# Recurrent states two half products apart, a split moved, and stores on another queue in a 2112-token hybrid layer

## The chip, the cores and the metric

The kernel runs on one core of one Trainium2 chip. Its engines work side by side, each through its own list of instructions: TensorE (PE, matrix products), VectorE (DVE), ScalarE (ACT), GpSimd (POOL), and SyncE (SP), which here only issues DMAs. ACT and POOL can issue DMAs as well. An instruction waits on semaphores for what it needs, and whatever stands behind it in its engine's list waits too. The metric is the device time of one execution in microseconds (us), as a median of several.

## The reference

One layer of a decoder with `d_model` 1024, in float32, for 2048 tokens of a prompt and 64 tokens of eight samples (2112 together). Two branches read the same input: sliding-window attention, and gated linear attention (GLA) with 4 heads of key width 128 and value width 256. The branches are projected, gated and added, projected once more, and normalised.

```
z = einsum('btd,dn->btn', x, w_in)
q, k, v, g_att, gq, gk, gv, g_gla, g_lr, r_att, r_gla = split(z)
o_att = sink_softmax(q k^T / 8 + rel_bias, window 128) v
log_a = log_sigmoid(g_lr @ w_gk_up + b_gk) / 16

# GLA, per head, in chunks of tokens; b = cumsum(log_a) in the chunk
o = (q exp(b)) S + tril((q exp(b)) (k exp(-b))^T) v
S = exp(b_last) S + (k exp(b_last - b))^T v

o = o * rsqrt(mean(o^2) + eps) * gla_norm_w
merged = sigmoid(r_att) * ((o_att * silu(g_att)) @ w_pa)
       + sigmoid(r_gla) * ((o * silu(g_gla)) @ w_pg)
y = layer_norm(DN_ALPHA * x + merged @ w_o)
```

Outputs are `y`, the last window of keys and values, and the GLA state after the prompt and after each sample.

## The kernel before

**Products.** A float32 operand is kept as two parts: `hi`, a cast to a shorter float type made on ACT (L123), and `lo`, the rest, subtracted on DVE (L124). A product is three matmuls (hi·hi, hi·lo, lo·hi) for each 128 rows of the contraction: L211 to L213 in the projections, L785 to L787 in the GLA, L1351 to L1353 in the merge. Names: `x` input, `wst` a raw weight and `wh`, `wl` its parts, `pd` and `pa` PSUM buffers, `wgk` the weights of the log gates.

**Stages** in the order of time, with the 2112 tokens in six chunks of 384 (four times), 256 and 320 (of it 64 samples):

- start, to about 100 us: first loads, splits, bias tables. `setup0` to `setup3` are its parts.
- attention, to about 397: per block of 128 queries scores, softmax, `att_trans` (transposes on PE, copied from PSUM into `pT`), `att_out`.
- GLA, about 357 to 1066, head after head, in each head chunk after chunk. The gate product z = `gin`·`wgk` (`gla_z`) opens a chunk; ACT and DVE make log gates, their running sum and four Exps of it from z (two table loads of ACT among them).
- merge, about 1066 to 1649: four passes of products over the branches (`w_pa`, `w_ra`, `w_rg`, `w_pg`), each by a seven-product scheme for 2×2 blocks, with 84 groups of matmuls. The third pass makes the GLA gates: PE, then DVE adds into `fin` (six buffers), then ACT's Tanh on it, then a store to `tt_d` in memory, which the fourth pass loads again as `cs`.
- output projection and norm, to the end.

**The recurrence.** A chunk has `nt` blocks of 128 tokens (3, or 2 in the last two chunks). Each goes through three parts. `gla_a`: scores (L763) and transpose of k (L764), then four casts or subtractions `ak` on ACT and DVE that split both. `gla_b`: the old state times q (L785 to L787 on `st`), the new state from `ak` and the values, the update on DVE (`ring`, L803), its split `st`, and the norm of the block's output (ACT square L777, POOL's `sq`, ACT scale L780). `gla_c`: two transposes of the normed output (L813), and the gating on DVE (L816). `samp_a`, `samp_b` and the "s" `gla_c` do the same for the samples of the last chunk, with states `S` that are loaded from `state` and stored to `o_ss`.

**What sets the order.** PE's list is in the order in which the program is written. The parts of the recurrence are put on a side list, `at(n, part)`, and are written out at the n-th next `tick()`; ticks stand between the dense products. In the first and third head (even) a tick is one full product of 24 matmuls. In the second and fourth (odd) a product has a tick in its middle too (`mid` in `proj`), so a tick is a half product of 12 matmuls, and a chunk has 8 of them: two gate products, k and q. `chain` says at which ticks the parts of a chunk stand. The fourth head's last two chunks are interleaved (`end`): that is its tail. The lists of ACT, DVE, POOL and SP are made by a scheduler that places each instruction by the order written and by when its inputs are due; `tc.issue_after` pins an instruction behind another. So a part that moves on PE takes its helpers on the other engines with it, and may land on the other side of unrelated work there.

Of the kernel before, what the change touches and what calls it, by code (L numbers as in the profile page):

```python
# [12 lines left out]
F32 = mybir.dt.float32  # L13
# [3 lines left out]
ALU = mybir.AluOpType  # L17
# [4 lines left out]
P = 128  # L22
# [4 lines left out]
NS = NB * TS  # L27
# [9 lines left out]
GH = 4  # L37
# [20 lines left out]
def kernel(ctx, tc, io):  # L58
# [47 lines left out]
    def at(d, fn):  # L106

        while len(side) <= d:
            side.append([])
        side[d].append(fn)  # L110
# [197 lines left out]
    def setup0():  # L308

        oneh = unit(name="oneh")  # L310
        rtab = small([33, NH], "rtab", 1)
        nc.gpsimd.memset(rtab, 1.0)
        nc.gpsimd.dma_start(oneh[:33, :LB], io["c_onehot"])
        nc.gpsimd.dma_start(rtab[:32], io["rel"])
        nc.gpsimd.dma_start(sink, io["sink"].broadcast_to([P, NH]))
        ssel = unit(name="ssel")[:NH, :2 * P].rearrange("h (a p) -> h a p", a=2)
        scol = small([NH, 1], "scol", 1)
        nc.gpsimd.dma_start(ssel, io["c_ssel"])
        nc.gpsimd.dma_start(scol, io["sink"].rearrange("a h -> h a"))
        oh = unit(F32R, "oh")[:33, :LB]  # L320
        rbh, rbl = (wtile(F32R, n).rearrange("p (h q) -> p h q", h=NH)[:33] for n in ("rbh", "rbl"))
        rt = rtab.unsqueeze(2).broadcast_to([33, NH, P])
        with tc.issue_after(pin["a"].ins), tc.issue_after(pin["d"].ins):
            nc.scalar.copy(wgk, wgk_st)
            nc.vector.tensor_tensor(wgk[64:], wgk_st[64:], wgk[64:].bitcast(F32), ALU.subtract)
            nc.scalar.copy(oh, oneh[:33, :LB])
            nc.vector.tensor_copy(rbh, rt)
            nc.vector.tensor_tensor(rbl, rt, rbh.bitcast(F32), ALU.subtract)
        st1.update(oh=oh, rbh=rbh, rbl=rbl, ssel=ssel, scol=scol)
# [30 lines left out]
            st1["bias", kv] = b  # L360

    def setup3():
        flat = bs_d.rearrange("h q j -> h (q j)")
        bias_s = unit(name="bias_s")[:, :2 * (W + TS)].rearrange("p (a k) -> p a k", a=2)
        for b in range(4):
            for h in range(NH):
                r = 32 * b + 8 * (h % G)
                f = flat[h, 127:127 + TS * (LB - 1)].rearrange("(q j) -> q j", j=LB - 1)
                nc.gpsimd.dma_start(bias_s[r:r + TS, h // G, :], f[:, :W + TS])
        st1["bias_s"] = bias_s  # L370
# [66 lines left out]
    def att_trans(A, bi, kv):  # L437
        first = A["kprev"] is None and bi == 0
        s = A.pop(("s", bi, kv))
        pT = wtile(name="pT").rearrange("p (a q) -> p a q", a=2)  # L440
        for hf in range(1 if first else 0, 2):
            tp = pa()
            for g in range(G):
                nc.tensor.transpose(tp[:, g * P:(g + 1) * P], s[:, g, hf * W:(hf + 1) * W], ident)
            nc.scalar.copy(pT[:, hf], tp)
        A["pT", bi, kv] = pT

    def att_out(A, bi):
# [122 lines left out]
    R = {}  # L571
# [10 lines left out]
    for c, (t0, T) in enumerate(CHUNKS):  # L582
# [2 lines left out]
        nblk = Tp // W  # L585
        if last:
            wcap(16)
        A = {"kprev": kprev, "vprev": vprev, "q": [], "sil": []}

        def wt1(key):  # L590
            if c == 0:
# [168 lines left out]
    def gla_a(B, i):  # L760
        ts = slice(i * P, (i + 1) * P)
        ap = pa()
        mm(ap[:, :P], B["k"][:, ts], B["q"][:, ts], start=True, stop=True)  # L763
        nc.tensor.transpose(ap[:, 256:256 + P], B["k2"][:, ts], ident)  # L764
        A_ = rot("a")
        nc.vector.copy_predicated(A_, cmask.bitcast(U32), ap[:, :P])
        As = rot("As")
        split(As[0], As[1], A_)
        kT2 = rot("kT")
        split(kT2[0], kT2[1], ap[:, 256:256 + P])  # L770
        B["a", i] = (As, kT2)
# [127 lines left out]
        for n_, x_ in ((0, x1), (2, x2)):  # L899
            nc.sync.dma_start(dst[n_:n_ + 2].rearrange("n p t -> p n t"), x_.rearrange("p (n t) -> p n t", n=2))  # L900

    def chain(B, o=0, late=False):

        last, nt = B["last"], B["nt"]
        if B["h"] == 0 and B["t0"] == 0:
            rings()
        short = nt == 2 and not last and o == 0
        end = last and B["h"] == GH - 1
        for i in range(nt):
            at(o + i, lambda B=B, i=i: gla_a(B, i))  # L910
            at((3, 5)[i] if short else o + i + 2, lambda B=B, i=i: gla_b(B, i))
            if not late:
                at((6, 7)[i] if short else o + i + 4, lambda B=B, i=i: gla_c(B, i, P, i * P))
        if last:
            at(o + nt + 2, lambda B=B: (nc.gpsimd if end else nc.sync).dma_start(
                io["o_sp"][B["h"]], R["S"][sstate[B["h"]]]))
            at(o + nt - 1, lambda B=B: samp_a(B))
            at(o + nt + 1, lambda B=B: samp_b(B, 0))
            at(o + nt + 2, lambda B=B: samp_b(B, 4))
            at(o + nt + 5, lambda B=B: gla_c(B, "s", NS, B["Tp"]))  # L920
            at(o + nt + 5, lambda B=B: gla_store(B))
        elif not late:
            at(7 if short else o + nt + 4 if o else 6, lambda B=B: gla_store(B))

    def values(B, i):

# [58 lines left out]
    for h in range(GH):  # L985
        W2 = {}
        odd = h % 2

        def wt2(*key):
            if key not in W2:  # L990
                W2[key] = wget()
            return W2[key]

        for c in range(len(CHUNKS)):
            last = c == LAST
            end = h == GH - 1 and c >= LAST - 1
            if not end:
                B = chunk(h, c, gin, gvn if odd else [])
            else:
                B = Bn  # L1000

            sums = [combine_load(stile)] if c else []
            if odd and c in (1, 2):
                sums.append(combine_load(lambda n: wtile(name=n)))

            def combine():
                if sums:
                    with tc.issue_after(pin["d"].ins):
                        combine_do(*sums.pop(0), nc.vector)

            def ahead():

                nh, nx = (h, c + 1) if not last else (h + 1, 0)
                if nh == GH:
                    return None, None, None
                g = gin5.pop() if gin5 else gate_in(nh, nx)
                return tiles(load_x(nx)), g, load_v(nh, nx) if nh % 2 else []

            if not odd:
                wv = [wt2("v", i) for i in range(4)]  # L1020
                if c == 0:
                    wcap(wseq[0] + 2)
                for i in range((B["T"] + P - 1) // P):
                    values(B, i)
                    if c == 0:
                        wload()
                    tick()
                if last:
                    wcap(wseq[0] + 4)
                    wload(2)  # L1030
            xn, gin, gvn = ahead()
            if odd and not end:
                if h < GH - 1 and c == 2:
                    wcap(wseq[0] + 6)
                for m in range(2):
                    gates(B, x, m, True)
                    if last:
                        wload()
                if 1 < c:
                    wload()  # L1040
            if h == GH - 1 and LAST - 2 <= c < LAST:
                Bn = chunk(h, c + 1, gin, gvn)
                if c == LAST - 2:
                    gin5.append(gate_in(h, LAST))
            dense(B, x, wt2("k"), gla_k, odd)
            combine()
            if not odd and last:
                wload()
            tick()
            dense(B, x, wt2("q"), gla_q, odd)  # L1050
            if not odd and last:
                wload()
            tick()
            combine()
            if end and not last:
                B["keep"] = wtile(name="keep")
                chain(B, 1, late=True)
                Bg, xg = B, x
            elif end:
                chain(B)  # L1060
                for m in range(2):
                    gates(B, x, m, True)
                for m in range(2):
                    gates(Bg, xg, m, True)
                for i in range(Bg["nt"]):
                    gla_c(Bg, i, P, i * P)
                drain()
                gla_store(Bg)
            else:
                if not odd:  # L1070
                    for m in range(2):
                        gates(B, x, m, False)
                chain(B, 1 if (h if not last else h + 1) % 2 else 0)
            x = xn


# [137 lines left out]

    def gate_sink(z, parts, ct, ts):
        nc.scalar.activation(z, z, AF.Tanh, scale=0.5)
        nc.sync.dma_start(tt_d[:, ct, 0, ts], z)

    def merge_sink(z, parts, ct, ts):
        nc.vector.scalar_tensor_tensor(z, parts[0], 1.0, z, ALU.add, ALU.mult)  # L1220
# [337 lines left out]
```

## Time and profile before

| | |
|---|---|
| median of 3 runs | 1852.0 us (1847.4 to 1854.77) |
| profiled execution | 1853.14 us |
| its span (first to last instruction) | 1851.4 us |
| granted TensorE clock | 0.991 |
| PE busy | 1806.5 us, 98% |
| DVE, ACT, POOL busy | 64%, 42%, 21% |
| DMA | mean 209 GB/s |

How to read it: a row of the timeline has the start and duration in us, the engine, the source line, the operation, `output<-input` by the program's names, shapes, and in square brackets the engine's idle time before it with what ended it. The rows of waits give the total, the number and the longest. A row of DMA issues gives the issuing engine's time; "to landing" is from the issue until the data has arrived. A releaser is inferred from semaphore events. Matmuls are pipelined and their ends are modelled, so two neighbours overlap in the list; the time from start to start is the measured one.

### The profile page before, as it was taken

What the parts mean: (1) busy time and instruction counts of PE and PEld (TensorE: products, weight loads), DVE (VectorE), ACT (ScalarE), POOL (GpSimd) and SP (SyncE); (2) the same over time, 40 slices, a digit from 0 to 9 for tenths busy, and PEclk for the clock granted to TensorE, in tenths of its full rate; (3) what the DMA queues carried; (4) which work ended last, traced back from release to release, by engine and by line L of the source; (5) the groups of instructions that cost most, each with busy time, mean ns of one, the idle gap of its engine ahead of it and who ended that gap; (6) DMA issues with size and microseconds to landing.
All of it is one profiled execution on the core that took longest, in us unless ns stands there. A gap on an engine that the chain in (4) does not pass through costs nothing. (4 is left out here: it accounts for less than half of the span.)

```text
span 1851.4 us, 29966 instructions
## 1 busy us (share of the span) xinstructions
PE 1806.5 (98%) x10883; PEld 1684.5 (91%) x10883; DVE 1177.9 (64%) x2433; ACT 784.3 (42%) x1762; POOL 381.6 (21%) x490
## 2 busy tenths in 40 slices
PE   7999999999999999999999899999999999999997
PEld 6988998989998998999999899999999999988886
DVE  5666767744456785444667669658657656966655
ACT  4444555633344564343546353435443543211100
POOL 2400000200001111000111243330355154631111
PEclk8999999999999999999999999999999999999999
DMA  8612233634457987444687589859787967895531
GB/s 270 233 53 92 75 107 118 200 134 145 135 198 255 327 285 251 168 163 145 224 310 248 195 278 294 282 178 298 256 301 263 307 221 244 283 312 188 161 108 50
DMA packets 194532, 386.70 MB, mean 209 GB/s; under 512 B 20557, under 2 KB 135077, under 8 KB 194368
## 3 DMA queue, kind: packets, MB, share of 16 engines
q1 hardware_dynamic: 190144, 378.43, 60.4%
q0 software_dynamic: 3088, 4.79, 0.8%
q8 instruction: 85, 1.39, 0.3%
q10 hardware_dynamic: 1152, 1.57, 0.3%
q14 instruction: 63, 0.52, 0.1%
HBM read 273.09 MB, written 112.62 MB: 208 GB/s over the span
## 5 line engine op out<-in xcount | busy, mean ns | idle before, releaser
L211 PE MATMUL pd<-x,wh 128*128 128x384 f32 (+2 forms) x1248 | 413.4, 331 | 8.1 <-ACT x L123 5.7
L213 PE MATMUL pd<-x,wl 128*128 128x384 f32 (+2 forms) x1248 | 404.6, 324 | 0.6 <-DVE wl L124 0.6
L212 PE MATMUL pd<-x,wh 128*128 128x384 f32 (+2 forms) x1248 | 404.8, 324 | 0.0
L1352 PE MATMUL pa<-xl,wh 128*128 128x352 f32 x1176 | 381.1, 324 | 9.6 <-DVE xl L124 9.3
L1351 PE MATMUL pa<-xh,wh 128*128 128x352 f32 x1176 | 381.8, 325 | 3.6 <-ACT xh L123 2.2
L1353 PE MATMUL pa<-xh,wl 128*128 128x352 f32 x1176 | 381.9, 325 | 0.0
L211 PEld LDWEIGHTS pd<-x,wh 128*128 128x128 f32 x1248 | 237.7, 190 | 18.6 <-ACT x L123 6.2
L212 PEld LDWEIGHTS pd<-x,wh 128*128 128x128 f32 x1248 | 237.5, 190 | 0.9 <-DVE x L124 0.8
L213 PEld LDWEIGHTS pd<-x,wl 128*128 128x128 f32 x1248 | 237.0, 190 | 1.0 <-DVE wl L124 1.0
L1352 PEld LDWEIGHTS pa<-xl,wh 128*128 128x128 f32 x1176 | 223.5, 190 | 12.6 <-DVE xl L124 12.6
L1351 PEld LDWEIGHTS pa<-xh,wh 128*128 128x128 f32 x1176 | 222.2, 189 | 4.9 <-ACT xh L123 2.4
L1353 PEld LDWEIGHTS pa<-xh,wl 128*128 128x128 f32 x1176 | 223.1, 190 | 0.2 <-DVE wl L124 0.2
L124 DVE TENSOR_TENSOR xl<-xs,xh 128x1408 fp32r<-128x1408 f32 x63 | 109.7, 1741 | 67.4 <-PE pa L1352 31.8
L778 POOL TENSOR_SCALAR sq<-sq 128x1 f32<-128x1 f32 (+1 forms) x68 | 20.4, 300 | 605.5 <-ACT ring L777 597.0
L123 ACT CAST xh<-xs 128x1408 fp32r<-128x1408 f32 x63 | 86.5, 1373 | 103.7 <-PE pa L1353 76.0
L224 PE MATMUL pd<-wh,x 128*128 128x512 f32 x256 | 101.7, 397 | 0.0
L226 PE MATMUL pd<-wol,x 128*128 128x512 f32 x256 | 101.5, 397 | 0.0
L225 PE MATMUL pd<-woh,x 128*128 128x512 f32 x256 | 101.5, 397 | 0.0
L224 PE MATMUL pd<-woh,x 128*128 128x512 f32 x256 | 101.5, 397 | 0.0
L226 PE MATMUL pd<-wl,x 128*128 128x512 f32 x256 | 99.8, 390 | 0.0
L123 ACT CAST x<-xst 128x384 fp32r<-128x384 f32 (+5 forms) x68 | 38.1, 570 | 145.7 <-PE pd L225 118.2
L225 PE MATMUL pd<-wh,x 128*128 128x512 f32 x256 | 99.8, 390 | 0.0
(340 smaller groups left out, 3337.2 us busy)
## 6 DMA issues: line engine op xcount, KB each, us to landing
x<-xs_d SPq DMA_DIRECT2D x64, 768.0 KB, 7.0
wst<-wt SPq DMA_DIRECT2D x33, 512.0 KB, 5.4
xs<-xc_d SPq DMA_DIRECT2D x24, 704.0 KB, 5.5
cs<-tt_d SPq DMA_DIRECT2D x48, 352.0 KB, 4.8
xs<-xT SPq DMA_DIRECT2D x18, 704.0 KB, 5.9
xs_d<-x SPq DMA_DIRECT2D x16, 768.0 KB, 5.0
x<-xs_d SPq DMA_DIRECT2D x16, 704.0 KB, 6.7
ws<-w_ra SPq DMA_DIRECT2D x36, 256.0 KB, 4.3
```

The source lines that it names most:

```text
L123: pin["a"] = nc.scalar.copy(dst_h, src)
L124: i = eng.tensor_tensor(dst_l, src, dst_h.bitcast(F32), ALU.subtract)
L211: mm(ps, hi[:, s], xh[:, :T], start=(k == 0), stop=False)
L212: mm(ps, hi[:, s], xl[:, :T], start=False, stop=False)
L213: mm(ps, lo[:, s], xh[:, :T], start=False, stop=(k == n - 1))
L224: mm(ps, xh[:, xs], hi, start=(k == 0), stop=False)
L225: mm(ps, xl[:, xs], hi, start=False, stop=False)
L226: mm(ps, xh[:, xs], lo, start=False, stop=(k == KT - 1))
L778: nc.gpsimd.tensor_scalar(sq[:n], sq[:n], EPS, None, op0=ALU.add)
L1351: mm(ps, wh[:, ks], xh[:, ts], start=(k == 0), stop=False)
L1352: mm(ps, wh[:, ks], xl[:, ts], start=False, stop=False)
L1353: mm(ps, wl[:, ks], xh[:, ts], start=False, stop=(k == q.kh - 1))
```

## The change

Four edits:

1. `chain` places the parts in the odd heads further apart: in a chunk of three blocks `gla_b` stands at ticks 3, 5 and 7 (before 3, 4, 5), `gla_a` at 1, 2 and 4 (before 1, 2, 3), `gla_c` two ticks behind its `gla_b`, and the store at 9 (before 8). For two blocks: a at 1 and 3, b at 4 and 6. The last chunk of an even head, whose parts stand between the next head's half products, has b at 3 and 5. The tail of the fourth head has its own table.
2. The split of the gate weights `wgk` is made in `setup3` and not in `setup0`, where it was pinned behind the first weight splits.
3. In `att_trans` the second half of each `pT`, 24 copies in the first four chunks, is copied by DVE and no longer by ACT.
4. In the third merge pass the 48 stores of gates are issued from ACT's queue and no longer from SP's.

```diff
@@ setup0
         with tc.issue_after(pin["a"].ins), tc.issue_after(pin["d"].ins):
-            nc.scalar.copy(wgk, wgk_st)
-            nc.vector.tensor_tensor(wgk[64:], wgk_st[64:], wgk[64:].bitcast(F32), ALU.subtract)
             nc.scalar.copy(oh, oneh[:33, :LB])
@@ setup3
     def setup3():
+        nc.scalar.copy(wgk, wgk_st)
+        nc.vector.tensor_tensor(wgk[64:], wgk_st[64:], wgk[64:].bitcast(F32), ALU.subtract)
@@ att_trans
-            nc.scalar.copy(pT[:, hf], tp)
+            if hf and A["c"] < len(CHUNKS) - 2:
+                nc.vector.tensor_copy(pT[:, hf], tp)
+            else:
+                nc.scalar.copy(pT[:, hf], tp)
@@ chain
-    def chain(B, o=0, late=False):
+    def chain(B, odd=False, tail=None):
...
+        if tail:
+            sa, sb_ = tail
+        elif not odd:
+            sa, sb_ = (0, 1, 2), (3, 5) if nt == 2 and not last else (2, 3, 4)
+        elif last:
+            sa, sb_ = (1, 2), (3, 5)
+        else:
+            sa, sb_ = ((1, 2, 4), (3, 5, 7)) if nt == 3 else ((1, 3), (4, 6))
+        n = sb_[nt - 1]
         for i in range(nt):
-            at(o + i, lambda B=B, i=i: gla_a(B, i))
-            at((3, 5)[i] if short else o + i + 2, lambda B=B, i=i: gla_b(B, i))
-            if not late:
-                at((6, 7)[i] if short else o + i + 4, lambda B=B, i=i: gla_c(B, i, P, i * P))
+            at(sa[i], lambda B=B, i=i: gla_a(B, i))
+            at(sb_[i], lambda B=B, i=i: gla_b(B, i))
+            if not (B["h"] == GH - 1 and B["c"] == LAST - 1):
+                at(sb_[i] + (3 if nt == 2 and not last and not odd and i == 0 else 2), lambda B=B, i=i: gla_c(B, i, P, i * P))
         if last:
-            at(o + nt + 2, lambda B=B: (nc.gpsimd if end else nc.sync).dma_start(
-                io["o_sp"][B["h"]], R["S"][sstate[B["h"]]]))
-            at(o + nt - 1, lambda B=B: samp_a(B))
-            at(o + nt + 1, lambda B=B: samp_b(B, 0))
-            at(o + nt + 2, lambda B=B: samp_b(B, 4))
-            at(o + nt + 5, lambda B=B: gla_c(B, "s", NS, B["Tp"]))
-            at(o + nt + 5, lambda B=B: gla_store(B))
-        elif not late:
-            at(7 if short else o + nt + 4 if o else 6, lambda B=B: gla_store(B))
+            at(n + 1, lambda B=B: (nc.gpsimd if end else nc.sync).dma_start(io["o_sp"][B["h"]], R["S"][sstate[B["h"]]]))
+            at(sa[-1 if tail else nt - 1], lambda B=B: samp_a(B))
+            at(n if tail or not odd else n + 1, lambda B=B: samp_b(B, 0))
+            at(n + (2 if odd else 1), lambda B=B: samp_b(B, 4))
+            at(n + 4, lambda B=B: gla_c(B, "s", NS, B["Tp"]))
+            at(n + 4, lambda B=B: gla_store(B))
+        elif not (B["h"] == GH - 1 and B["c"] == LAST - 1):
+            at(n + 2, lambda B=B: gla_store(B))
@@ the calls of chain
-                chain(B, 1, late=True)
+                chain(B, tail=((3, 5), (5, 7)))
...
-                chain(B)
+                chain(B, tail=((1, 3), (4, 6)))
...
-                chain(B, 1 if (h if not last else h + 1) % 2 else 0)
+                chain(B, (h + last) % 2 == 1)
@@ gate_sink
-        nc.sync.dma_start(tt_d[:, ct, 0, ts], z)
+        nc.scalar.dma_start(tt_d[:, ct, 0, ts], z)
```

What this makes of the engines' lists, at the three places that the prediction speaks of. First ACT in the second head, from the first activation on z of its fourth chunk (line numbers behind the edit are higher by 3 in the changed kernel: L780 here is L777 before, L783 is L780). Before:

```order
L720 ACTIVATE ga<-pd,bgk 128x384
L722 ACTIVATE ga<-ga 128x384
L723 ACT_TABLE_LOAD
L723 ACTIVATE ga<-ga 128x384
L123 CAST ak<-aper_193 128x128
L123 CAST ak<-pa 128x128
L737 ACT_TABLE_LOAD
L737 ACTIVATE em<-dm 128x384
L738 ACTIVATE ek<-ek 128x384
L739 ACTIVATE dm<-dm 128x384
L740 ACTIVATE gb<-gb 128x384
L246 ACTIVATE th<-pd 128x384
```

And now:

```order
L723 ACTIVATE ga<-pd,bgk 128x384
L783 ACTIVATE ring<-pa,sq 128x256
L123 CAST st<-ring 128x256
L725 ACTIVATE ga<-ga 128x384
L726 ACT_TABLE_LOAD
L726 ACTIVATE ga<-ga 128x384
L740 ACT_TABLE_LOAD
L740 ACTIVATE em<-dm 128x384
L741 ACTIVATE ek<-ek 128x384
L742 ACTIVATE dm<-dm 128x384
L743 ACTIVATE gb<-gb 128x384
L246 ACTIVATE th<-pd 128x384
```

The next two rows are now the `ak` casts of the first block, which before stood ahead of the second table load, and the norm and state cast of the previous chunk's last block (`ring`, `st`) now stand inside this row of activations.

Second, DVE at the hand-over from the GLA to the merge, whose first product is split into `xh` and `xl`. Before:

```order
L872 SCALAR_TENSOR_TENSOR S_11479<-S_11479,e_11122,pa 128x256 x4
L816 SCALAR_TENSOR_TENSOR sg<-pa,nw_h,sg 128x128
L247 SCALAR_TENSOR_TENSOR sg<-th,pd 128x256
L816 SCALAR_TENSOR_TENSOR sg<-pa,nw_h,sg 128x128
L816 SCALAR_TENSOR_TENSOR sg<-pa,nw_h,sg 128x64
L247 SCALAR_TENSOR_TENSOR sg<-th,pd 128x256
L816 SCALAR_TENSOR_TENSOR sg<-pa,nw_h,sg 128x64
L816 SCALAR_TENSOR_TENSOR sg<-pa,nw_h,sg 128x128 x4
L124 TENSOR_TENSOR xl<-xc_11704,xh 128x704
```

And now:

```order
L806 SCALAR_TENSOR_TENSOR ring<-ring,e_11115,pa 128x256
L875 SCALAR_TENSOR_TENSOR S_11506<-S_11506,e_11117,pa 128x256 x4
L247 SCALAR_TENSOR_TENSOR sg<-th,pd 128x256
L875 SCALAR_TENSOR_TENSOR S_11508<-S_11508,e_11117,pa 128x256 x4
L819 SCALAR_TENSOR_TENSOR sg<-pa,nw_h,sg 128x128 x6
L819 SCALAR_TENSOR_TENSOR sg<-pa,nw_h,sg 128x64 x2
L124 TENSOR_TENSOR xl<-xc_11704,xh 128x704
```

Four updates of `S` and eight gatings now stand between the last gate (`sg<-th`) and the first `xl`; before, five gatings did.

Third, the stores of the third merge pass. Before, in SP's list, between loads of weights (`ws`) and inputs (`xs`):

```order
L1124 DMA ws<-w_rg 128x512 x4
L1155 DMA xs<-xc_d 128x1408
L1124 DMA ws<-w_rg 128x512 x6
L1217 DMA tt_d<-fin 128x352
L1124 DMA ws<-w_rg 128x512
L1155 DMA xs<-xc_d 128x1408
L1217 DMA tt_d<-fin 128x352 x2
```

And now, in ACT's list:

```order
L123 CAST xh<-xs 128x1408
L1227 ACTIVATE fin<-fin 128x352
L1228 DMA tt_d<-fin 128x352
L1227 ACTIVATE fin<-fin 128x352
L1228 DMA tt_d<-fin 128x352
L1227 ACTIVATE fin<-fin 128x352
L1228 DMA tt_d<-fin 128x352
L123 CAST xh<-xs 128x1408
```

Each store has left SP and stands directly behind its Tanh on ACT.

More of the change, by code (lines that the diff above doesn't have):

```diff
@@ L587 @@
             wcap(16)
-        A = {"kprev": kprev, "vprev": vprev, "q": [], "sil": []}
+        A = {"c": c, "kprev": kprev, "vprev": vprev, "q": [], "sil": []}
         def wt1(key):
@@ L906, in chain @@
             rings()
-        short = nt == 2 and not last and o == 0
         end = last and B["h"] == GH - 1
+        if tail:
[7 more added lines that the diff above has]
+        n = sb_[nt - 1]
         for i in range(nt):
-            at(o + i, lambda B=B, i=i: gla_a(B, i))
-            at((3, 5)[i] if short else o + i + 2, lambda B=B, i=i: gla_b(B, i))
-            if not late:
-                at((6, 7)[i] if short else o + i + 4, lambda B=B, i=i: gla_c(B, i, P, i * P))
+            at(sa[i], lambda B=B, i=i: gla_a(B, i))
+            at(sb_[i], lambda B=B, i=i: gla_b(B, i))
+            if not (B["h"] == GH - 1 and B["c"] == LAST - 1):
+                at(sb_[i] + (3 if nt == 2 and not last and not odd and i == 0 else 2), lambda B=B, i=i: gla_c(B, i, P, i * P))
         if last:
-            at(o + nt + 2, lambda B=B: (nc.gpsimd if end else nc.sync).dma_start(
-                io["o_sp"][B["h"]], R["S"][sstate[B["h"]]]))
-            at(o + nt - 1, lambda B=B: samp_a(B))
-            at(o + nt + 1, lambda B=B: samp_b(B, 0))
-            at(o + nt + 2, lambda B=B: samp_b(B, 4))
-            at(o + nt + 5, lambda B=B: gla_c(B, "s", NS, B["Tp"]))
-            at(o + nt + 5, lambda B=B: gla_store(B))
-        elif not late:
-            at(7 if short else o + nt + 4 if o else 6, lambda B=B: gla_store(B))
+            at(n + 1, lambda B=B: (nc.gpsimd if end else nc.sync).dma_start(io["o_sp"][B["h"]], R["S"][sstate[B["h"]]]))
[6 more added lines that the diff above has]
+            at(n + 2, lambda B=B: gla_store(B))
     def values(B, i):
```

## Prediction

> **What bounds the kernel now.** I read the page first, then the busy time by stage, then the waits of TensorE (PE), and only then the timelines around the waits that the change can touch. In the page, the span and the busy times:
>
> ```profile
> span 1851.4 us, 29966 instructions
> PE 1806.5 (98%) x10883; PEld 1684.5 (91%) x10883; DVE 1177.9 (64%) x2433; ACT 784.3 (42%) x1762; POOL 381.6 (21%) x490
> ```
>
> PE is busy for 98%. None of the four edits changes the number of matmuls, so the change can win only what PE waits, and lose only what it makes PE wait. By stage (us, busy time and instructions of each engine, granted clock, DMA share, GB/s): second head, third head, fourth head in two pieces, then the third merge pass.
>
> ```profile
> 577.00:706.00 129.00, 127.36 (x851) 123.43 (x850) 94.47 (x250) 74.55 (x179) 17.50 (x38) 1.00 0.92 311
> 706.00:921.00 215.00, 215.00 (x1241) 196.32 (x1240) 108.01 (x275) 87.51 (x215) 16.09 (x36) 1.00 0.51 179
> 921.00:1014.00 93.00, 92.04 (x583) 88.78 (x582) 64.00 (x174) 52.66 (x128) 11.55 (x25) 1.00 0.81 284
> 1014.00:1066.00 52.00, 45.72 (x332) 42.27 (x332) 33.36 (x107) 21.84 (x66) 10.63 (x22) 0.97 0.59 201
> 1314.00:1479.00 165.00, 162.44 (x1008) 161.65 (x1007) 95.80 (x125) 76.56 (x122) 70.13 (x54) 1.00 0.83 284
> ```
>
> The third head waits for nothing (215.00 of 215.00). The second loses 1.6 us, the fourth 1.0 and then 6.3 in its tail, the third merge pass 2.6. These bracket the prize: some 11.5 us, 0.6% of the kernel. Who ends the waits (total, times, longest):
>
> ```profile
> PE pa L1352 <- DVE xl L124: 9.3, 8, 2.2
> PE pa L785 <- ACT ak L123: 3.1, 1, 3.1
> PE pa L785 <- ACT st L123: 2.7, 5, 1.1
> PE pd L211 <- DVE qb L402: 1.5, 1, 1.5
> PE pa L340 <- DVE rbl L328: 1.3, 1, 1.3
> PE pa L786 <- DVE st L124: 0.8, 3, 0.5
> PE pa L1351 <- DVE fin L1185: 0.8, 1, 0.8
> PE pa L862 <- DMA S<-state: 0.6, 1, 0.6
> PE pa L813 <- ACT ring L780: 0.4, 1, 0.4
> ```
>
> `st` is the recurrent state cast for the next block: it, `ring` and `S` are the waits that spreading the recurrence should remove, 2.7 + 0.8 + 0.4 + 0.6 = 4.5 us. `ak` is another cause. The idle column understates such a wait, since a matmul's modelled end runs on after the next could start:
>
> ```profile
> 1042.39 0.38 PE L785 MATMUL pa<-st,qih 128*128 128x256 f32 x1 [1.08 <-ACT st L123]
> 1042.85 0.39 PE L786 MATMUL pa<-st,qih 128*128 128x256 f32 x1
> 1043.07 0.28 PE L787 MATMUL pa<-st,qil 128*128 128x256 f32 x1
> 1043.19 0.28 PE L785 MATMUL pa<-gv,ak 128*128 128x256 f32 x1
> ```
>
> The undisturbed pitch of these is 0.12 (1043.07 to 1043.19); the next two starts took 0.46 and 0.22, so 0.34 and 0.10 were lost beyond the 1.08, and start to start the place lost 1.7. I therefore use lost start-to-start time below, about twice the idle column for short waits.
>
> **Recurrences.** The change puts two half products between a state and its next use, where before there was one. A half product of 12 matmuls takes about 2.1 us at 384 columns (starts 0.17 to 0.18 apart around 657), against `st` waits of at most 1.1, so I count every such wait as gone. Start to start, at the places of the `st`, `ring` and `S` rows above: last chunk of the first head (591 and 594) 0.8, and 0.8 for `S`, which is used a tick later; second head (666, 684, 699) 1.9; last chunk of the third (935) 0.8; fourth head 4.6, of it 0.9, 1.7 and 1.6 at 1029, 1042 and 1052 in its tail. Sum **−8.9**, bounded by −4.5 (idle column) and −8.9.
>
> What is late next is ScalarE (ACT). The gate's z matmul of one chunk of the second head on PE, and then the timeline of ACT:
>
> ```profile
> 648.60 0.44 PE L718 MATMUL pd<-gin,wgk 96*128 96x384 f32 x1
> ...
> 654.54 1.28 ACT L737 ACT_TABLE_LOAD   x1
> 657.88 0.29 ACT L123 CAST ak<-aper 128x128 fp32r<-128x128 f32 x1
> 658.06 0.26 ACT L123 CAST ak<-pa 128x128 fp32r<-128x128 f32 x1
> 662.88 1.05 ACT L123 CAST wh<-wst 128x1024 fp32r<-128x1024 f32 x1 [1.16 <-DMA wst<-wt]
> ```
>
> Before, the first `ak` casts of the chunk stand ahead of that table load; in the changed order they stand behind it, four Exps and a `th`, where this timeline has the second pair: 657.88 to 658.32, that is z + 9.7. I put the block product that needs it at z + 9.2 by counting products from z. With 0.1 to 0.2 to the matmul that is a wait of about 0.75 in four chunks, little in three, and 1.9 in the last chunk of the second head, where a `wh` cast of 1.05 is ahead as well. The norm of the block before now also stands between these activations. Sum **+5.3** over 8 chunks; lower bound 0 (all a little earlier than I count), upper bound 3.1 each, from the one place where this very queueing is on PE's path already:
>
> ```profile
> 1017.41 1.28 ACT L723 ACT_TABLE_LOAD   x1
> 1018.70 0.47 ACT L723 ACTIVATE ga<-ga 128x320 f32<-128x320 f32 x1
> 1021.20 1.28 ACT L737 ACT_TABLE_LOAD   x1 [2.02 <-issue]
> 1024.13 0.25 ACT L123 CAST ak<-pa 128x128 fp32r<-128x128 f32 x1
> ```
>
> This is the `ak` wait of 3.1: both table loads, a wait for the scan and five activations lie ahead of the casts. The change leaves it. I take a value near the lower bound, since here ACT waited 2.02 for the scan before the table load and PE had only 320 columns a matmul to fill the time; at 654.54 the load waited for nothing.
>
> The Trainium skill, page "ScalarE: Activation LUTs", section "What ACT_TABLE_LOAD costs", gives 1.28 us for a table load and another 1.38 for a drain at each switch, which would speak against putting casts behind it. The trace agrees on 1.28 and shows no drain: the load of 1017.41 ends when the next activation starts. With a drain, 8 chunks would cost an estimated 11 us more and the time would be some 1859.
>
> **Hand-over to the merge.** The waiting matmul on PE, and VectorE (DVE) ahead of it:
>
> ```profile
> 1067.61 0.42 PE L1352 MATMUL pa<-xl,wh 128*128 128x352 f32 x1 [1.12 <-DVE xl L124]
> 1059.70 1.64 DVE L872 SCALAR_TENSOR_TENSOR S<-S,e,pa 128x256 f32<-128x256 f32 x4
> 1065.45 1.31 DVE L816 SCALAR_TENSOR_TENSOR sg<-pa,nw_h,sg 128x64 f32<-128x64 f32 x5
> 1066.68 0.88 DVE L124 TENSOR_TENSOR xl<-xc,xh 128x704 fp32r<-128x704 f32 x1
> ```
>
> The first `xl` comes after the fourth head's last work on DVE. In the changed order four `S` updates (1.64) and eight instead of five gated copies stand between the last gate and `xl`, so `xl` comes some 5.8 us after the last product and not 2.9; of these 2.9, PE covers about 1.2 with matmuls that now also come last. **+1.7**, between 0 and 2.7 (with a slower clock behind a longer gap).
>
> **Gates of the third pass.** DVE stops for 5.7 and 4.7 us because all `fin` buffers wait for their stores, which stand on SyncE's (SP) queue behind weight loads that wait for their own buffers:
>
> ```profile
> 1355.41 0.52 DVE L1185 TENSOR_TENSOR fin<-a,pa 128x352 f32<-128x352 f32 x1 [5.72 <-DMA tt_d<-fin]
> 1342.85 9.22 SPq L1124 DMA_DIRECT2D ws<-w_rg  x6
> 1352.12 0.42 SPq L1217 DMA_DIRECT2D tt_d<-fin  x1
> L1217 SPq DMA_DIRECT2D tt_d<-fin x24: 319/418/884, 1352.1 to 1439.9; - x24
> DMA to landing us min/median/max: 2.5/5.0/8.2
> ```
>
> PE pays the `fin` wait of 0.8 and two `xl` waits of 1.7 behind it, start to start 3.3. From ACT's queue a store is issued right behind its Tanh. The 48 issues take 0.42 each at the median, 20 us on an engine that is busy 76.56 of 165, in front of casts that PE needs. I count **−3.3 and +1.0**: between −3.3 and +3, the latter if a queue on ACT backs up as SP's does (up to 0.88 an issue).
>
> The Trainium skill, page "DMA: Bandwidth & Descriptors", section "Issuing engines are not separate DMA queues", says that a second issuing engine saves issue time alone, since the same 16 engines do the work. Here the store waited 9.22 on SP before any DMA engine had it, so the trace shows a larger saving on the way to the queue. By the rule alone the pass would gain nothing, and the time would be 1851.
>
> **The two small edits.** The split of the gate weights stood ahead of the `rbl` that PE waits 1.3 for. It isn't later: nothing pins it now, and the new order has it ahead of the first weight casts, in an idle time of ACT and DVE. **−0.2**, between −1.3 and +0.6 (one cast, below). In the attention 24 copies of half a transposed block go from ACT to DVE:
>
> ```profile
> L324 ACT CAST wgk<-wgk_st x1: 615/615/615, 27.5 to 27.5; 96x512 fp32r<-96x512 f32 x1
> L445 ACT COPY pT<-pa x62: 568/588/607, 80.6 to 384.9; 128x512 f32<-128x512 f32 x62
> ```
>
> That is 24 × 0.588 = 14 us in some 300 on an engine that has a third of its time free; PE's only wait there is the 1.5 for `qb`. **0**, between −1.5 and +1.5: if the cover fails, a transposed half is late by one DVE operation.
>
> **Sum.** −8.9 + 5.3 + 1.7 − 3.3 + 1.0 − 0.2 + 0 = −4.4. The profiled execution took 1853.1 (span 1851.4), 1.1 above the median of 1852.0, so 1848.7 in its terms and **1848** as a median of runs. A measurement of this kernel (1847.4 to 1854.8 unchanged) can't tell less than about 0.5%, 9 us, from nothing: faster is below 1842.7, slower above 1861.3.
>
> **Rivals.**
> - *The spreading is free.* `ak` comes in time everywhere, the hand-over is covered and ACT takes the stores: −8.9 − 3.3 − 0.2 and a little from the faster clock, −13, 1839. For it: casts at z + 9.7 against a need that I know to some 0.5 us. Against it: the order of ACT is worse for `ak` in all 8 chunks, and the first store queued on ACT stands ahead of casts.
> - *ACT's order makes every odd chunk late.* The place is the second and fourth head, between z and the first block product; the price 3.1 each, as at 1024.13, when the `wh` casts wait for weights (1.16 at 662.88; the DMA engines are at 0.92) or the scan comes late. 8 × 3.1 is 24.8 for my 5.3: +15 in all, 1867. It loses against before from 1.2 us a chunk, by over 0.5% from 2.4. Against it: in the trace the second pair ran at z + 9.7 with the same activations ahead.
> - *The stores gain nothing* (ACT is held by its issues, or the landing of 5.0 is what counts): 1848 + 2.3, 1850 or 1851; no other sign.
> - *The recurrences don't wait for spacing at all:* what stays are casts queued on ACT behind a gate. Then the 8.9 shrinks to half, the new costs stay: 1853.
>
> **Chances.** Forecast 0.45, free spreading 0.25, late chunks 0.10, stores gain nothing 0.12, spacing not the cause 0.08. The three that lie around 1848 to 1853 are all within 0.5%: 0.65. Range 1838 to 1858: it holds all but half of the late chunks' mass and a part of the free case; the forecast's own range is 1842 to 1855.
>
> **What would show it.** Right: in the profile after, no wait of the state's product (L785 before) on `st` in the second and fourth head; new waits of the block products on `ak` of 0.2 to 1.9 in chunks of the second and fourth head; the 3.1 near 1024 still there; L1352's first wait on `xl` longer than 1.1; no `fin` wait on `tt_d` in the third pass. Wrong: `ak` waits over 2 in most odd chunks, waits of PE on ACT casts in the third pass, or a new wait in the attention on a `pT` of DVE.

## The result

The changed kernel takes **1860.4 us** (median of 16 runs, 1854.8 to 1865.0) against 1851.7 for the kernel before (16 runs, 1847.4 to 1855.9): a ratio of **1.0047, 95% interval 1.0035 to 1.0060**, so 8.7 us slower. The forecast was 1848 and the range ended at 1858.

The profiled execution took 1858.6, a little below its median. Its span, busy times, and the waits of PE by who ended them (total, times, longest):

```profile
span 1856.9 us, 29958 instructions
PE 1806.5 (97%) x10883; PEld 1682.8 (91%) x10883; DVE 1192.6 (64%) x2457; ACT 771.8 (42%) x1738; POOL 378.2 (20%) x490
```

```profile
PE pa L1363 <- DVE xl L124: 13.5, 8, 3.7
...
PE pa L1362 <- ACT xh L123: 4.7, 4, 1.7
PE pa L788 <- ACT ak L123: 4.2, 4, 3.2
...
PE pa L338 <- DVE rbl L326: 1.3, 1, 1.3
...
PE pa L816 <- ACT ring L783: 0.9, 2, 0.7
...
PE pa L789 <- DVE st L124: 0.6, 1, 0.6
PE pd L213 <- DVE wl L124: 0.6, 1, 0.6
PE pd L721 <- DMA gin<-gl_d: 0.6, 1, 0.6
```

PE's busy time is 1806.5 in both kernels, by chance: with the same 10883 matmuls it lies between 1801.4 and 1810.1 in the profiled executions of this document. The waits on `st` that the new ticks were to remove fell from 3.5 us (2.7 and 0.8) to 0.6. The `ak` waits rose from 3.1 to 4.2, as forecast in kind. What was not forecast is in the first two rows shown: the waits for split inputs of the merge, 9.3 and 2.2 before, are 13.5 and 4.7. Of this rise of 6.7, 4.4 fall in the third pass.

Taking each stage from the start of its first matmul to the start of the next stage's, in the two profiled executions (us):

| stage | before | after | |
|---|---|---|---|
| start and attention, to the first z | 352.9 | 352.2 | −0.7 |
| second head's first chunk (with the end of the first head) | 27.2 | 25.1 | −2.1 |
| rest of the second head, to the third's second z | 142.5 | 145.5 | +3.1 |
| fourth head's first chunk (with the end of the third) | 26.0 | 25.1 | −0.9 |
| rest of the fourth head, to its last z | 67.0 | 67.8 | +0.9 |
| tail and first merge pass | 138.2 | 138.6 | +0.4 |
| second pass | 161.8 | 160.3 | −1.5 |
| **third pass** | **165.3** | **171.4** | **+6.1** |
| fourth pass to its last product | 172.8 | 171.7 | −1.1 |
| output | 187.8 | 189.6 | +1.8 |

The rest of the first and third head took the same in both.

The third pass, where 3.3 were to be won, lost 6.1. Its row of the busy times (before: 162.44 for the 1008 matmuls at a granted clock of 1.00):

```profile
1314.00:1485.00 171.00, 164.93 (x1008) 163.87 (x1007) 95.16 (x125) 75.36 (x120) 67.58 (x52) 0.98 0.80 270
```

So PE's idle time in the pass grew by 3.6 (2.5 before, 6.1 now), and the same 1008 matmuls took 2.5 longer at a granted clock of 0.98. The slower stretch lies directly behind the longest wait: from 1355.57 to 1360.55 matmuls start 0.29 apart on average, where the median of the pass is 0.16.

### The profile page after: what moved, and what is told of

Its sections match the earlier page's. It is cut to its first block, busy times and chain, and to the rows that moved or that the text cites. A ratio compares the mean times of both kernels' runs of the same rounds, so it can differ in the third digit from the quotient of the medians.

```text
span 1856.9 us, 29958 instructions
## 1 busy us (share of the span) xinstructions
PE 1806.5 (97%) x10883; PEld 1682.8 (91%) x10883; DVE 1192.6 (64%) x2457; ACT 771.8 (42%) x1738; POOL 378.2 (20%) x490
## 4 chain that ended last, share of the span: by engine, by line
PE 80%; DMA 7%; DVE 5%; ACT 3%; issue 2%; POOL 2%; SPq 0%; DVEq 0%; ACTq 0%; POOLq 0%
PE pd L211 9%; PE pd L213 9%; PE pd L212 9%; PE pa L1363 7%; PE pa L1364 7%; PE pa L1362 7%; PE pd L226 6%; PE pd L224 6%; PE pd L225 6%; DMA cs<-tt_d 2%; PE pa L459 2%; PE pa L444 1%; PE pa L790 1%; PE pa L789 1%; PE pa L788 1%
## 5 line engine op out<-in xcount | busy, mean ns | idle before, releaser
L1363 PE MATMUL pa<-xl,wh 128*128 128x352 f32 x1176 | 381.3, 324 | 13.8 <-DVE xl L124 13.5
L124 DVE TENSOR_TENSOR wl<-ws,wh 128x512 fp32r<-128x512 f32 (+1 forms) x108 | 84.8, 796 | 26.3 <-ACT wh L123 25.9
L224 PE MATMUL pd<-wh,x 128*128 128x512 f32 x256 | 101.7, 397 | 0.0
```

Of the source, the lines that this page charges most:

```text
L124: i = eng.tensor_tensor(dst_l, src, dst_h.bitcast(F32), ALU.subtract)
L224: mm(ps, xh[:, xs], hi, start=(k == 0), stop=False)
L1363: mm(ps, wh[:, ks], xl[:, ts], start=False, stop=False)
```

## What holds ScalarE in the third pass

ACT's timeline in the changed kernel at the start of the third pass. `ACTq` rows are the issues of stores, a bracket is ACT's idle time ahead of an instruction:

```profile
1339.28 1.37 ACT L123 CAST xh<-xs 128x1408 fp32r<-128x1408 f32 x1
1340.55 0.50 ACT L1227 ACTIVATE fin<-fin 128x352 f32<-128x352 f32 x1
1345.96 0.34 ACTq L1228 DMA_DIRECT2D tt_d<-fin  x1
1346.35 0.50 ACT L1227 ACTIVATE fin<-fin 128x352 f32<-128x352 f32 x1 [5.30 <-DMA ws<-w_rg]
1348.98 0.33 ACTq L1228 DMA_DIRECT2D tt_d<-fin  x1
1349.36 0.50 ACT L1227 ACTIVATE fin<-fin 128x352 f32<-128x352 f32 x1 [2.51 <-DMA ws<-w_rg]
1350.51 0.33 ACTq L1228 DMA_DIRECT2D tt_d<-fin  x1
1350.93 1.37 ACT L123 CAST xh<-xs 128x1408 fp32r<-128x1408 f32 x1 [1.08 <-DMA ws<-w_rg]
```

The first Tanh ends at 1341.05, and its result could be stored. The store is issued at 1345.96, and what releases it is a weight load, `ws<-w_rg`, which has nothing to do with `fin`. The cast `xh` that the next product needs stands two stores further back and runs at 1350.93. DVE's `xl` follows from it, and PE pays:

```profile
1352.33 2.72 DVE L124 TENSOR_TENSOR xl<-xs,xh 128x1408 fp32r<-128x1408 f32 x1 [8.04 <-ACT xh L123]
```

```profile
1352.35 0.43 PE L1362 MATMUL pa<-xh,wh 128*128 128x352 f32 x1 [0.99 <-ACT xh L123]
1355.11 0.66 PE L1363 MATMUL pa<-xl,wh 128*128 128x352 f32 x1 [2.32 <-DVE xl L124]
```

Why a weight load releases a store stands in the program's lists, when the semaphores that a row waits for are printed with it. Three stores of ACT:

```
L1228 DMA tt_d<-fin 128x352 [waits DMAHW3_49,Activation_49]
L1228 DMA tt_d<-fin 128x352 [waits DMAHW6_49,Activation_49]
L1228 DMA tt_d<-fin 128x352 [waits DMAHW1_49,Activation_49]
```

The framework gives the DMAs of SP's and ACT's queues together eight completion semaphores in rotation, in the order in which its scheduler placed them. The trace agrees: the 1108 DMAs of the two queues name the same eight semaphores, 138 or 139 each, and ahead of each of these stores ACT waits for the semaphore that the store itself will use. In this program a DMA may use its semaphore again only when the DMA eight places earlier has landed, so its issue waits for that one, whichever queue it was on. On SP such a wait holds other DMAs. On ACT it holds casts. Laying the order of the program over the trace gives, for each store, when the DMA eight places earlier was issued and landed:

| store issued | DMA eight places earlier | it was issued | it landed | from landing to the store |
|---|---|---|---|---|
| 1345.96 | `ws<-w_rg` (SP) | 1339.26 | 1345.89 | 0.07 |
| 1348.98 | `ws<-w_rg` (SP) | 1344.10 | 1348.90 | 0.08 |
| 1350.51 | `ws<-w_rg` (SP) | 1344.95 | 1350.44 | 0.07 |
| 1354.84 | `ws<-w_rg` (SP) | 1348.28 | 1354.76 | 0.08 |
| 1358.02 | `xc<-ug_d` (SP) | 1349.59 | 1357.95 | 0.07 |
| 1358.92 | `tt_d<-fin` (ACT) | 1350.51 | 1357.74 | 1.18 |
| 1360.55 | `ws<-w_rg` (SP) | 1353.60 | 1360.48 | 0.07 |

Of the first 12 stores (to 1376) 11 are issued 0.07 to 0.08 after that landing, so the semaphore is what they waited for; of the other 36 only 6 are.

## The experiments

Theory A is the one above. Theory B: the recurrences and the hand-over cost the time, and the stores only shift a wait. Theory C: the issues take ACT's time, 0.33 each. Theory D: a second issuing engine beside SP is a cost by its traffic. Each run stands against the kernel before, timed beside it on the same chip: 1850.6 beside the first four runs, 1848.2 beside the next four and 1851.6 beside the last.

**The stores back on SP, all else changed.**

```diff
-        nc.scalar.dma_start(tt_d[:, ct, 0, ts], z)
+        nc.sync.dma_start(tt_d[:, ct, 0, ts], z)
```

> The changed kernel with the 48 gate stores of the third merge pass back on SP's queue, all else kept. Theory A (a store on ACT is held until the DMA that used its completion semaphore before has landed, and holds the casts behind it): the third pass takes 165.3 us from its first matmul to the fourth pass's first, as before (171.4 in the changed kernel), and the time is 1860.4 - 6.1 = 1854, within 2. Theory B (the spread recurrences and the hand-over are what costs, the stores only shift a wait): 1858 or more.

1850.4 us, ratio 0.9995 (0.9984 to 1.0005): the loss is gone. By the medians it is 10.0 (1860.4 to 1850.4) and not the 6.1 of the profile, so the time lies below the 1854, within 2, that I expected. The third pass took 162.3, where 165.3 was expected, and PE's waits in it are

```profile
PE pa L1363 <- DVE xl L124: 0.6, 1, 0.6
```

**The stores on ACT, all else as before.**

```diff
-        nc.sync.dma_start(tt_d[:, ct, 0, ts], z)
+        nc.scalar.dma_start(tt_d[:, ct, 0, ts], z)
```

> The kernel before with only the 48 gate stores of the third merge pass moved to ACT's queue. Theory A: the third pass lengthens by about 6 us, ACT idles up to 5 us in front of a store issue that ends 0.1 us after a load on the same semaphore has landed; time 1852 + 6 = 1858, within 2. Theory B: 1852, within 1.

1860.1, ratio 1.0051 (1.0035 to 1.0067). The one line makes the whole loss, so theory B is out. The profiled third pass took 168.9; ACT in it shows the same picture:

```profile
1343.10 0.49 ACT L1216 ACTIVATE fin<-fin 128x352 f32<-128x352 f32 x1
1348.15 0.34 ACTq L1217 DMA_DIRECT2D tt_d<-fin  x1
1348.53 0.50 ACT L1216 ACTIVATE fin<-fin 128x352 f32<-128x352 f32 x1 [4.94 <-DMA ws<-w_rg]
```

Here too 11 of the first 12 stores are issued 0.07 to 0.08 after the landing eight places earlier.

**The new ticks alone.** The edit is the `chain` part of the change, as shown above, and its three calls.

> The kernel before with only the new tick table of the recurrences. From the two profiles, stage by stage: first chunk of the second head -2.1, rest of it +2.4 and 0.6, fourth head's first chunk -0.9 and rest +0.9, tail and hand-over with the first merge pass +0.4. Theory A: +1.3 in all, 1853, within 2. Theory B: +6 or more, 1858.

1851.8, ratio 1.0005 (0.9994 to 1.0017): no difference that can be measured. From the second head's first z to the end of the first merge pass the five kernels with all the new ticks took 573.8 to 577.1 (mean 576.0), the five with the old ones 573.9 to 575.4 (mean 574.7). So what the ticks win at the first chunks they lose again, and 1.4 us more on average, though the two groups overlap.

**The two small edits alone** (the split of `wgk` and the copies on DVE, as in the change).

> The kernel before with only the split of the gate weights moved and the 24 copies of half a transposed block on DVE. Both theories: the start is about 0.75 us shorter up to the first gate product and nothing else moves: 1851, within 1. If the copies on DVE delay anything, it shows as a wait of PE between 100 and 400 us.

1849.3, ratio 0.9998 (0.9988 to 1.0007). In the attention, from 100 to 400 us, PE shows no wait at all, here as in the changed kernel. Up to the first z the six kernels with these edits took 351.5 to 353.2 (mean 352.3), the five without 352.9 to 354.7 (mean 353.8): in the direction of the 0.75 expected, and too little to be seen in the total.

**Twelve stores, or thirty-six.** Theories A and C both put the cost on ACT; they differ in which stores carry it. The first 12 stores are those of one block of the four, which this condition picks out:

```diff
-        nc.sync.dma_start(tt_d[:, ct, 0, ts], z)
+        (nc.scalar if ct % 2 == 0 and ts.start // T % 2 == 0 else nc.sync).dma_start(tt_d[:, ct, 0, ts], z)
```

> The kernel before with only the first 12 of the 48 gate stores of the third merge pass on ACT's queue, the other 36 on SP's. In the trace of the changed kernel 11 of these 12 are issued 0.07 to 0.08 us after the landing of the DMA eight places earlier, on the same completion semaphore, up to 4.9 us after the store was ready. Theory A (semaphore in rotation): all of the loss is here; 1851 + 8 = 1859, within 2. Theory C (the issues themselves take ACT's time, 0.33 each, so the loss goes with their number): a quarter of the loss, 1853.

1858.0, ratio 1.0062 (1.0045 to 1.0079), with the third pass at 170.1: twelve stores cost as much as forty-eight. The reverse, with `nc.sync` and `nc.scalar` exchanged in that line:

> The reverse of the run above: the first 12 gate stores on SP, the other 36 on ACT. Theory A: few of these 36 find their semaphore taken when a cast is due; 1851, within 2, and the third pass takes 162 to 166 us. Theory C: three quarters of the loss, 1858.

1850.1, ratio 1.0006 (0.9993 to 1.0018), third pass 163.7. Thirty-six issues cost nothing that can be measured, so theory C is out. PE's waits in the third pass of the two, first the twelve, then the thirty-six:

```profile
PE pa L1352 <- DVE xl L124: 4.5, 3, 2.0
PE pa L1351 <- ACT xh L123: 1.9, 1, 1.9
```

```profile
PE pa L1352 <- DVE xl L124: 1.5, 2, 0.8
```

The difference of the two groups is in their surroundings. The first 12 fall where SP issues the pass's weight loads, inputs and recombination loads one behind the other, each 4 to 8 us from issue to landing (1337 to 1360 in the changed kernel), so the DMA eight places back is still in flight when the store is ready. In the changed kernel 29 of the other 36 are issued 0.2 us or more after it has landed. That the stores slow the loads by their traffic in this crowded stretch does not show: SP's loads issued from 1337 to 1360 take a median of 6.2 us to land in the kernel before, 6.5 in the changed kernel and 5.2 in the run with twelve.

**The stores on POOL's queue**, which has semaphores of its own:

```diff
-        nc.scalar.dma_start(tt_d[:, ct, 0, ts], z)
+        nc.gpsimd.dma_start(tt_d[:, ct, 0, ts], z)
```

> The changed kernel with the 48 gate stores issued by POOL, whose queue has other completion semaphores and no casts that PE waits for. Theory A: stores no longer hold ACT, and are not behind SP's loads either: third pass 162 to 165 us, time 1850 to 1852 (1849 if the fin waits go altogether). Theory D (more than one issuing engine is itself the cost, by traffic that runs beside the loads): near the changed kernel, 1858 or more.

1860.6, ratio 1.0069 (1.0050 to 1.0087), where I expected 1850 to 1852: the third pass took 177.3, the longest of all. Theory D would have it so, but the trace names another reason: the stores stand in POOL's list too, and there they are behind sums of weights that wait for their own inputs. The first store is issued 10.4 us after its Tanh has ended (1344.29 to 1354.70), so `fin` isn't given back, DVE waits for it, and PE for DVE:

```profile
1353.46 1.29 POOL L1144 TENSOR_TENSOR ws<-ws 128x512 f32<-128x512 f32 x1
1354.70 0.56 POOL L1228 DMA_DIRECT2D tt_d<-fin  x1
1355.28 1.30 POOL L1145 TENSOR_TENSOR ws<-ws 128x512 f32<-128x512 f32 x1
```

```profile
1362.91 0.52 DVE L1196 TENSOR_TENSOR fin<-a,pa 128x352 f32<-128x352 f32 x1 [11.08 <-DMA tt_d<-fin]
```

```profile
PE pa L1362 <- DVE fin L1196: 7.2, 3, 3.2
```

The run shows another way to lose the same time, and so decides nothing between A and D; the run with the 36 stores does, since there ACT and SP both issue, at no cost.

**The old ticks where the new ones lost.** On top of the stores on SP, the odd heads' ordinary chunks get back the ticks that they had, and only the ends of the even heads and the tail are spread:

```diff
-            sa, sb_ = ((1, 2, 4), (3, 5, 7)) if nt == 3 else ((1, 3), (4, 6))
+            sa, sb_ = (1, 2, 3), (3, 4, 5)
```

> The changed kernel with the stores on SP and, in the odd heads' ordinary chunks, the old ticks (blocks at 3, 4, 5); the spreading is kept in the last chunks of the even heads and in the fourth head's tail, where it gained. From the profiles: the second head's later chunks 2.4 us and the fourth head's 0.5 shorter than with the spreading; the first chunks' gains of 2.1 and 0.9 stay. Time 1850.4 - 3 = 1847, within 2, faster than both kernels.

1849.1, ratio 1.0003 (0.9989 to 1.0016): not the 3 us that I expected. The stretch from the second head's first z to the end of the first merge pass took 575.5, within the range of both groups above; the gain of the ends (2.1 and 0.9) is there, but the rest of the second head still took 144.3, 1.8 more than before, and the tail with the first pass 139.7, 1.5 more. A version that beats the kernel before clearly was not found.

**Stores on ACT, but later.** The same 48 issues on ACT, held back and issued four at a time behind the next input cast (`pin["a"]` is the last cast of a split on ACT):

```diff
+    late = []
+
+    def flush():
+        with tc.issue_after(pin["a"].ins):
+            while late:
+                d, z = late.pop(0)
+                nc.scalar.dma_start(d, z)
+
     def gate_sink(z, parts, ct, ts):
         nc.scalar.activation(z, z, AF.Tanh, scale=0.5)
-        nc.scalar.dma_start(tt_d[:, ct, 0, ts], z)
+        late.append((tt_d[:, ct, 0, ts], z))
...
         make_x(n + 1)
+        if late:
+            flush()
         make_w(n)
```

> The changed kernel, its 48 gate stores still on ACT's queue, but held back and issued four at a time, behind the input cast (xh) of the next unit and the unit's last Tanh, instead of each right behind its Tanh. The number of issues and their bytes are the same. Theory A (what costs is that a store waits for its semaphore in front of the casts): the casts are ahead now and the semaphore's earlier DMA has had longer to land; most of the 9 to 10 us come back: third pass 162 to 166 us, time 1850 to 1853; with six fin buffers a fin wait on DVE may keep 2 to 3. Theory D (a second issuing engine beside SP is the cost in itself): the changed kernel's time, 1858 to 1860.

1855.4, ratio 1.0024 (1.0010 to 1.0038): by the medians half of the loss comes back, less than I expected, and the interval just overlaps that of the changed kernel (from 1.0035). The profiled third pass took 169.1, where 162 to 166 was expected: 2.3 less than in the changed kernel and within the range of the kernels that lose. ACT still waits at the issues, now with the cast ahead of them:

```profile
1344.07 1.38 ACT L123 CAST xh<-xs 128x1408 fp32r<-128x1408 f32 x1
1345.35 0.49 ACT L1235 ACTIVATE fin<-fin 128x352 f32<-128x352 f32 x1
1351.20 6.93 ACTq L1232 DMA_DIRECT2D tt_d<-fin  x4
1358.18 0.88 ACT L1235 ACTIVATE fin<-fin 128x352 f32<-128x352 f32 x2 [12.34 <-DMA tt_d<-fin]
```

The four issues are 0.07 to 0.08 behind the landings of four of SP's loads (1351.13, 1351.81, 1354.61, 1357.73), so the wait for the semaphore is as long as before. What it delays has changed: the input cast is spared, and the later Tanhs and the `fin` buffers pay (DVE waits 10.9 for one). That the time moved with what stands behind the issue, at the same number of issues and bytes, fits theory A better than C or D, but with so small a difference it would not decide alone; the runs with twelve and with thirty-six stores do.

## Why the prediction was wrong

**The step that failed** is the term "−3.3 and +1.0" for the gates of the third pass, "between −3.3 and +3". It is +9.5 by the medians (1860.1 against 1850.6 with this line alone). Both of its halves failed:

- *The gain of 3.3.* I read that the stores waited on SP behind weight loads, and took it that "from ACT's queue a store is issued right behind its Tanh". It is not: it has to wait for its semaphore, and that belongs to one of the very loads it was to get past. The stores did come sooner (the first six 0.0 to 4.9 us after their Tanh, on SP 8.1 to 10.4), and the wait that the gain was read from is gone: the first row below, of the kernel before (1310 to 1480), has no counterpart in the changed kernel. But what is left of the wait now holds the casts, and PE waits longer for those. That could be seen beforehand: the second row, also of the kernel before, has two stores that were released by a load of `xs`, with which they share nothing but a semaphore.

```profile
DVE fin L1185 <- DMA tt_d<-fin: 10.9, 3, 5.7
SPq L1217 <- DMA xs<-xc_d: 2.7, 2, 1.9
```

- *The cost of 1.0.* I priced an issue at its 0.42 and "backing up" at 0.88. The price of an issue on a compute engine is not its own duration but the longest wait that it can carry, and everything in that list pays it. Here that was up to 4.9 us, in front of the cast that PE needs.

The prediction had named the sign of it, "waits of PE on ACT casts in the third pass", which are 2.5 us now and were none before; the most it allowed for them was the 3 at the end of the term's range.

The Trainium skill, page "DMA: Bandwidth & Descriptors", section "Issuing engines are not separate DMA queues", had it that a second issuing engine saves issue time alone. Its sum, 1851, was nearer than mine, and the runs show a cost beyond it. I set it aside with SP's 9.22; but that row is six issues of loads with SP's waits among them, and of the 8.9 that the first store itself waited on SP, 4.9 were left on ACT. The Trainium skill, page "DMA: Bandwidth & Descriptors", section "Anatomy of one DMA — SWDGE (gpsimd) path", says that a semaphore wait happens on the issuing sequencer before the DMA is dispatched. The trace agrees (0.07 to 0.08 from the landing to the issue), and by that sentence a store on ACT was worth pricing by its waits.

**The recurrences** went as the steps said, with errors of size. The `st` waits are gone but for 0.6. The `ak` wait near 1024 stayed (3.1, now 3.2). The new waits came where they were put, four chunks at about 0.6 each for the 0.75 forecast, and 1.1 in the last chunk of the second head for the 1.9:

```profile
633.62 0.39 PE L788 MATMUL pa<-gv,ak 128*128 128x256 f32 x1 [0.16 <-ACT ak L123]
633.84 0.28 PE L789 MATMUL pa<-gv,ak 128*128 128x256 f32 x1
634.26 0.39 PE L790 MATMUL pa<-gv,ak 128*128 128x256 f32 x1
...
1024.63 0.39 PE L788 MATMUL pa<-gv,ak 128*128 128x256 f32 x1 [3.16 <-ACT ak L123]
```

Beyond them there were waits I had not counted, on the norm (`ring`, 0.9 start to start near 681), on `st` from DVE (0.9 near 686) and on `gin` (0.75 near 1003). My −8.9 + 5.3 + 1.7 was −1.9 for the stretch; the run with the new ticks alone gives +0.9, with an interval of −1.1 to +3.1. So the sum was about 3 us too good (0.8 to 5.0 by that interval), by terms on both sides that nearly cancel. The rival "spacing is not the cause" was wrong in its mechanism, since the `st` waits did go, and near in its time by luck.

**The hand-over** was right in its mechanism: `xl` comes after four updates of `S` and eight gatings, and PE waits 2.2 for it instead of 1.1, so 1.1 more for the 1.7 forecast:

```profile
1061.87 1.65 DVE L875 SCALAR_TENSOR_TENSOR S<-S,e,pa 128x256 f32<-128x256 f32 x4
1063.44 2.02 DVE L819 SCALAR_TENSOR_TENSOR sg<-pa,nw_h,sg 128x128 f32<-128x128 f32 x8
1065.37 0.88 DVE L124 TENSOR_TENSOR xl<-xc,xh 128x704 fp32r<-128x704 f32 x1
```

**The small edits** were right in size: the split runs earlier, at 21.4 us and not 27.5, and the copies on DVE are covered; together 0.9998. But the wait that the first of the two terms named, PE's 1.3 for `rbl`, is still 1.3.

**The rivals.** The one on the other side ("ACT's order makes every odd chunk late") named the wrong stage. It had the right kind of mechanism, work that PE needs queued on ACT behind something that waits for a DMA, and I didn't ask where else the change puts such a thing. "The stores gain nothing" had "ACT is held by its issues" as its reason, and priced it with 2.3.

**What stays open.** In profiled executions the third pass with the first 12 stores on ACT (168.9 to 171.4 in three kernels) is 6.7 longer on average than with all on SP (162.3 to 165.3 in five). The medians differ by 9 to 10. A profiled execution is one of many (these eight lay from 5.1 below to 1.4 above the medians of their kernels), so a few us of the difference aren't placed in any stage.

## What to carry to other kernels

A DMA issued from an engine that computes brings its waits into that engine's list: before moving one there, print what it waits for, find when that is met, and ask which instruction stands behind it. Semaphores that several queues share in rotation, as the eight here, make a transfer wait for unrelated ones, and moving it to another of these queues does not get it past them. Whether the stall on `fin` can be removed by giving the buffer back earlier in SP's own queue was not tried.

## What was not expected of the hardware

An issue that waits shows as idle time of its engine, and the profile puts it on the next instruction, with the unrelated DMA as the releaser (5.30 ahead of a Tanh "<- DMA ws<-w_rg"). From the landing to the issue that it allows takes 0.07 to 0.08 us. Behind PE's longest wait of the third pass matmuls started 0.29 apart and not 0.16, so the wait cost more than its own length. And 36 issues of 0.33 on an engine that is busy for less than half of the stage cost nothing that can be measured (1.0006), while 12 in the wrong place cost 0.6%.
